# Weight sums of a seven-product block multiplication, made by accumulating transfers

## The chip, the cores and the metric

The kernel runs on one NeuronCore of a Trainium2 chip (trn2). The metric is device time in microseconds of one execution; the median of three runs is compared. The engines are TensorE (PE, with its weight loads shown as PEld), VectorE (DVE), ScalarE (ACT), GpSimd (POOL) and SyncE (SP). Each works through its own queue of instructions in order and waits on semaphores for the others. Transfers are issued by SP, ACT or POOL.

## The reference

One decoder block on x of 512 tokens by 1024 features, in float32: a SwiGLU feed-forward, a token mixer (a gated linear recurrence beside a sliding-window attention), and a second SwiGLU, each with a norm before and behind it.

```python
def swiglu(x, w_gu, w_down):
    g, u = jnp.split(x @ w_gu, 2, axis=-1)
    return (jax.nn.silu(g) * u) @ w_down
...
f = swiglu(rms_norm(h, ffn1_pre_g[l]), ffn1_w_gu[l], ffn1_w_down[l])
h = h + MACARON_SCALE * rms_norm(f, ffn1_post_g[l])
m = hybrid_mixer(rms_norm(h, mix_pre_g[l]), ...)
h = h + rms_norm(m, mix_post_g[l])
f = swiglu(rms_norm(h, ffn2_pre_g[l]), ffn2_w_gu[l], ffn2_w_down[l])
h = h + MACARON_SCALE * rms_norm(f, ffn2_post_g[l])
```

The feed-forward width D_FF is 2816, so `w_gu` is 1024 by 5632. Only the product `x @ w_gu` of the two feed-forwards is touched by the change.

## The kernel before, in words

A float32 product is made of three TensorE products in the type float32r: every operand is split into a high part (a cast to float32r) and a low part (the operand less the high part), and `mm3` (lines 130 to 132) adds high by high, high by low and low by high. ScalarE makes the high parts, VectorE the low parts. A product thus needs the high part of its weights for its first two matmuls and the low part from the third on.

The 22 chunks of 128 gate columns and 128 up columns are made in order. The first 6 chunks of the first feed-forward (names begin with f1) and the first 4 of the second (f2) go through ordinary products of 512 tokens. The rest goes through `paired`, which is where the change lies. `paired` takes a 2 by 2 block form of the multiplication: the features halved on one side, two chunks of 128 columns on the other, and the tokens halved. Seven block products instead of eight give the four result blocks (the form of Strassen and Winograd). The combinations of the moving side (tokens) are made once, in `moving` and `scaled`, and lie in `mv[1]` to `mv[7]`. The combinations of the weights are made for every pair k, from four raw blocks of 128 by 512.

A pair k of chunks is one period. There are n = 16 periods in f1 (an even k makes the gate columns of two chunks, the odd k behind it their up columns) and 18 in f2. A block product is 12 matmuls of 128 by 128 weights on 256 tokens: 4 feature blocks times the three of `mm3`. A period has 7 of them, so 84 matmuls.

In the kernel before, `load(k)` brings the raw blocks as two tiles, L and R (two blocks each, 512 KB each, by SP). `sums(k)` makes four sums on VectorE: M (two blocks), N, and a new first block of L. `parts(k, w)` splits R, M, L and N (w = 1 to 4) into high and low. `product(i, k, start)` issues product i into the PSUM bank X, Y or Q of pair k. Products 1, 6, 3 or 5 and others accumulate on top of each other in one bank, so between them a copy of the bank is taken: `snap` is a ScalarE copy of 256 columns, and `add` is the VectorE addition of such a copy to another bank. `finish` applies the SwiGLU: on an even k (gate) a tanh on ScalarE and a combination on VectorE, on an odd k (up) the multiplication.

`period(k)` is written out by hand and stands under `tc.manual_schedule()`, so the order of the text is what each engine's queue is given. In it products 1, 2, 6 and 7 belong to pair k, and products 5, 3 and 4 to pair k - 1: their weights (parts 3 and 4) are made at the end of a period and used in the next. The low and high parts lie in tiles of the pool `big` (19 buffers), the raw tiles and the part N in `t4p` (8 buffers).

Of the kernel before, what the change touches and what calls it, by code (L numbers as in the profile page):

```python
# [8 lines left out]
F32 = mybir.dt.float32  # L9
# [29 lines left out]
def hybrid_block_kernel(ctx, tc, x, xt, g1, w_first, gains, gu1, gs1, dn1, w_x, w_gate, w_q, w_k, w_v, w_gl, w_ga, w_pl, w_pa,  # L39
# [254 lines left out]
    def paired(fast, name, ps):  # L294
        src, mv = fast
        n = src.shape[0]
        st = [{} for _ in range(n)]
        lo_, hi_ = slice(0, 256), slice(256, 512)

        def load(k):  # L300
            if k < n:
                st[k]["L"], st[k]["R"] = (t4(f"{name}{z}{k}").rearrange("p (a b) -> p a b", a=2) for z in "LR")
                for i, z in ((1, "L"), (0, "R")):
                    SP.dma_start(st[k][z].rearrange("p a b -> p (a b)"), src[k, i])

        def sums(k):
            d = st[k]
            L, R = d["L"], d["R"]
            d["M"] = M = t4(f"{name}M{k}").rearrange("p (a b) -> p a b", a=2)
            d["N"] = N = t2(f"{name}N{k}")  # L310
            for o, a, b in ((M[:, 1], R[:, 1], L[:, 0]), (L[:, 0], L[:, 0], L[:, 1]), (M[:, 0], R[:, 1], L[:, 0]),
                            (N, R[:, 0], M[:, 0])):
                V.tensor_tensor(out=o, in0=a, in1=b, op=ALU.add)

        def parts(k, w):
            d = st[k]
            raw = d["RMLN"[w - 1]]
            if w == 4:
                d["W4"] = t4(f"{name}W4{k}", F32R).rearrange("p (s b) -> p s b", s=2)
            else:  # L320
                d[f"W{w}"] = b8(f"{name}W{w}{k}", [P, 2, 2, 512], F32R)
            t = d[f"W{w}"]
            A.copy(t[:, 0], raw)
            V.tensor_tensor(out=t[:, 1], in0=raw, in1=t[:, 0].bitcast(F32), op=ALU.subtract)  # L324

        def product(i, k, start):
            d = st[k]
            o = d[" XYXQXXQ"[i]][:, lo_]
            w, slot = {1: (1, 1), 2: (1, 0), 3: (4, None), 4: (3, 1), 5: (3, 0), 6: (2, 0), 7: (2, 1)}[i]
            t = d[f"W{w}"]  # L330
            wh, wl = (t[:, 0], t[:, 1]) if slot is None else (t[:, 0, slot], t[:, 1, slot])
            bh, bl = mv[i]
            for k4 in range(4):
                ks = slice(k4 * P, (k4 + 1) * P)
                mm3(o, wh[:, ks], wl[:, ks], bh[:, k4, :], bl[:, k4, :], start and k4 == 0, k4 == 3, True)

        def snap(k, key):
            d = st[k]
            if key == "s1":
                d["sn"] = t2(f"{name}sn{k}")  # L340
                d["s1"], d["s2"] = d["sn"][:, lo_], d["sn"][:, hi_]
            if key == "sW":
                d["sW"] = t2(f"{name}sw{k}")[:, lo_]
            A.copy(d[key], d["X"][:, lo_])  # L344

        def add(k, key):
            d = st[k]
            if key == 11:
                d["a"], d["b"] = t2(f"{name}ca{k}"), t2(f"{name}cb{k}")
                V.tensor_tensor(out=d["a"][:, lo_], in0=d["Y"][:, lo_], in1=d["s1"], op=ALU.add)  # L350
            elif key == 22:
                V.tensor_tensor(out=d["b"][:, hi_], in0=d["Q"][:, lo_], in1=d["sW"], op=ALU.add)
            else:
                V.tensor_tensor(out=d["b"][:, lo_], in0=d["Q"][:, lo_], in1=d["s2"], op=ALU.add)

        def finish(k):
            d = st[k]
            a, b, X = d["a"], d["b"], d["X"][:, lo_]
            j = JSTD[name] + k // 2 * 2
            if k % 2 == 0:  # L360
                d["ta"], d["tb"] = t2(f"{name}ta{k}"), t2(f"{name}tb{k}")
                ta, tb = d["ta"], d["tb"]
                A.activation(ta[:, lo_], a[:, lo_], AF.Tanh, scale=0.5)
                A.activation(ta[:, hi_], X, AF.Tanh, scale=0.5)
                A.activation(tb, b, AF.Tanh, scale=-0.5)
                for o, z in ((ta[:, lo_], a[:, lo_]), (ta[:, hi_], X), (tb, b)):
                    V.scalar_tensor_tensor(out=o, in0=o, scalar=1.0, in1=z, op0=ALU.add, op1=ALU.mult)
            else:
                ta, tb = st[k - 1]["ta"], st[k - 1]["tb"]
                if j % 4 == 0:  # L370
                    ps.append(b8(f"{name}p{j // 4}", [P, 4, T]))
                pa, pb = ps[-1][:, j % 4, :], ps[-1][:, j % 4 + 1, :]
                for o, t, z in ((pa[:, lo_], ta[:, lo_], a[:, lo_]), (pa[:, hi_], ta[:, hi_], X), (pb, tb, b)):
                    V.scalar_tensor_tensor(out=o, in0=t, scalar=0.5, in1=z, op0=ALU.mult, op1=ALU.mult)

        for k in range(3):
            load(k)
        sums(0)
        parts(0, 1)
        parts(0, 2)  # L380

        def period(k):
            c, o, d = k < n, k - 1, k + 1
            if k >= 2:
                add(k - 2, 21)
                finish(k - 2)
            if d < n:
                sums(d)
                parts(d, 1)
# [4 lines left out]
            if o >= 0:  # L394
                product(5, o, False)
            if c:
                snap(k, "s1")
                add(k, 11)
            if o >= 0:
                snap(o, "sW")  # L400
                add(o, 22)
            if c:
                product(6, k, False)
                product(7, k, True)
                if d < n:
                    parts(d, 2)
                snap(k, "s2")
            if o >= 0:
                product(3, o, False)
                product(4, o, False)  # L410
            if c:
                parts(k, 3)
                parts(k, 4)
# [4 lines left out]
            load(k + 3)  # L418
# [575 lines left out]
```

## Time and profile before

| | |
|---|---|
| median of three runs | 1159.44 us (1159.2 to 1159.59) |
| span of the profiled execution | 1158.4 us (its own time beside the span is not on the page) |
| mean granted TensorE clock | 0.995 |
| paired stage of f1 | first matmul 76.9 us, last near 251.5 us |
| paired stage of f2 | first matmul 849.8 us, last near 1036.5 us |
| accumulating transfers, transfers issued by POOL | none |

A row of the timeline reads: start and length in us, engine, line, operation, tile written <- tiles read, sizes, and in brackets the idle time of that engine just before and what ended it. Tile names leave out the numbers: f1X is bank X of any pair, f2W any weight part. A group row has the count behind x, then busy us and the mean in ns of one instruction, then the idle time before them. A row of the transfers ends with the size and the median time from issue to landing. TensorE's instructions overlap: the distance between two starts is the real pace, not the length.

### The profile page before, as it was taken

What the parts mean: (1) busy time and instruction counts of PE and PEld (TensorE: products, weight loads), DVE (VectorE), ACT (ScalarE), POOL (GpSimd) and SP (SyncE); (2) the same over time, 40 slices, a digit from 0 to 9 for tenths busy, and PEclk for the clock granted to TensorE, in tenths of its full rate; (3) what the DMA queues carried; (4) which work ended last, traced back from release to release, by engine and by line L of the source; (5) the groups of instructions that cost most, each with busy time, mean ns of one, the idle gap of its engine ahead of it and who ended that gap; (6) DMA issues with size and microseconds to landing.
All of it is one profiled execution on the core that took longest, in us unless ns stands there. A gap on an engine that the chain in (4) does not pass through costs nothing.

```text
span 1158.4 us, 16623 instructions
## 1 busy us (share of the span) xinstructions
PE 1132.6 (98%) x6680; PEld 1008.4 (87%) x6680; DVE 804.2 (69%) x1182; ACT 537.3 (46%) x924; POOL 57.4 (5%) x58
## 2 busy tenths in 40 slices
PE   7979999999999999999999999999999999999997
PEld 6769999998888988887888888888999999998886
DVE  6598898984415887999877562546769898874303
ACT  7334555553313667566555341425435454553301
POOL 1000000000001010113121000000000000000000
PEclk9999999999999999999999999999999999999999
DMA  9113333284213453622822340624223333274011
GB/s 362 45 66 110 110 110 108 81 297 151 79 54 116 177 139 116 184 72 58 246 84 89 125 163 20 208 83 147 72 74 109 105 101 100 80 272 158 7 37 72
DMA packets 40604, 138.61 MB, mean 120 GB/s; under 512 B 4944, under 2 KB 5072, under 8 KB 39888
## 3 DMA queue, kind: packets, MB, share of 16 engines
q1 hardware_dynamic: 35920, 122.35, 32.4%
q10 hardware_dynamic: 4608, 15.21, 3.7%
q8 instruction: 52, 0.85, 0.3%
q14 instruction: 24, 0.20, 0.1%
HBM read 126.01 MB, written 11.53 MB: 119 GB/s over the span
## 4 chain that ended last, share of the span: by engine, by line
PE 87%; DVE 9%; ACT 2%; issue 2%; DMA 1%; POOL 0%; DVEq 0%; POOLq 0%; ACTq 0%
PE f1o L130 3%; PE f2o L130 3%; PE f1o L132 3%; PE f2o L132 3%; PE f1o L131 3%; PE f2o L131 3%; PE f2X L131 3%; PE f2X L132 3%; PE f2X L130 3%; PE f1X L130 3%; PE f1X L132 3%; PE f1X L131 3%; PE f1f L574 2%; PE f2Q L132 1%; PE f2Q L131 1%
## 5 line engine op out<-in xcount | busy, mean ns | idle before, releaser
L101 DVE TENSOR_TENSOR w<-wraw,w 128x1024 fp32r<-128x1024 f32 x128 | 155.7, 1244 | 67.0 <-ACT w L100 65.6
L100 ACT CAST w<-wraw 128x1024 fp32r<-128x1024 f32 x128 | 129.3, 1049 | 99.7 <-PE f1o L132 17.7
L130 PE MATMUL f1X<-u1m,f1W 128*128 128x256 f32 x256 | 73.1, 286 | 3.7 <-ACT f1sn L344 3.7
L132 PE MATMUL f1X<-u1m,f1W 128*128 128x256 f32 x256 | 73.2, 286 | 2.3 <-DVE f1W L324 2.3
L131 PE MATMUL f1X<-u1m,f1W 128*128 128x256 f32 x256 | 73.0, 285 | 0.0
L130 PE MATMUL f2o<-w,f2ph 128*128 128x512 f32 x176 | 68.6, 390 | 0.0
L130 PE MATMUL f1o<-w,f1ph 128*128 128x512 f32 x176 | 68.5, 390 | 0.0
L131 PE MATMUL f1o<-w,f1ph 128*128 128x512 f32 x176 | 68.5, 389 | 0.0
L131 PE MATMUL f2o<-w,f2ph 128*128 128x512 f32 x176 | 68.5, 389 | 0.0
L132 PE MATMUL f1o<-w,f1pl 128*128 128x512 f32 x176 | 67.0, 389 | 0.0
L132 PE MATMUL f2o<-w,f2pl 128*128 128x512 f32 x176 | 66.9, 389 | 0.0
L130 PEld LDWEIGHTS f1X<-u1m,f1W 128*128 128x128 f32 x256 | 49.6, 194 | 4.0 <-ACT f1sn L344 3.9
L132 PEld LDWEIGHTS f1X<-u1m,f1W 128*128 128x128 f32 x256 | 49.6, 194 | 2.6 <-DVE f1W L324 2.5
L131 PEld LDWEIGHTS f1X<-u1m,f1W 128*128 128x128 f32 x256 | 49.7, 194 | 0.1
L132 PE MATMUL f2X<-u3h,f2W 128*128 128x256 f32 x144 | 40.8, 283 | 0.0
L130 PE MATMUL f2X<-u3m,f2W 128*128 128x256 f32 x144 | 40.8, 283 | 0.0
L131 PE MATMUL f2X<-u3m,f2W 128*128 128x256 f32 x144 | 40.8, 283 | 0.0
L130 PE MATMUL f2Q<-u3m,f2W 128*128 128x256 f32 x144 | 40.8, 283 | 0.0
L131 PE MATMUL f2Q<-u3m,f2W 128*128 128x256 f32 x144 | 40.8, 283 | 0.0
L132 PE MATMUL f2Q<-u3m,f2W 128*128 128x256 f32 x144 | 40.8, 283 | 0.0
L131 PE MATMUL f2X<-u3l,f2W 128*128 128x256 f32 x144 | 40.8, 283 | 0.0
L132 PE MATMUL f2X<-u3m,f2W 128*128 128x256 f32 x144 | 40.7, 283 | 0.0
(722 smaller groups left out, 3519.9 us busy)
## 6 DMA issues: line engine op xcount, KB each, us to landing
wraw<-in_dn_dram SPq DMA_DIRECT2D x44, 512.0 KB, 4.7
f2L<-in_gs_dram SPq DMA_DIRECT2D x18, 512.0 KB, 3.6
f2R<-in_gs_dram SPq DMA_DIRECT2D x18, 512.0 KB, 4.4
wraw<-in_gu_dram SPq DMA_DIRECT2D x16, 512.0 KB, 5.8
f1L<-in_gs_dram SPq DMA_DIRECT2D x16, 512.0 KB, 3.6
f1R<-in_gs_dram SPq DMA_DIRECT2D x16, 512.0 KB, 4.4
wraw<-in_w_x_dram SPq DMA_DIRECT2D x8, 512.0 KB, 4.5
wraw<-in_w_q_dram SPq DMA_DIRECT2D x8, 512.0 KB, 4.4
```

Of the source, the lines that this page charges most:

```text
L100: A.copy(w[:, 0, :], raws[n])
L101: V.tensor_tensor(out=w[:, 1, :], in0=raws[n], in1=w[:, 0, :].bitcast(F32), op=ALU.subtract)
L130: PE.matmul(o, lhsT=ah, rhs=bh, start=start, stop=False, skip_group_check=reopen)
L131: PE.matmul(o, lhsT=ah, rhs=bl, start=False, stop=False, skip_group_check=reopen)
L132: PE.matmul(o, lhsT=al, rhs=bh, start=False, stop=stop, skip_group_check=reopen)
L574: PE.matmul(bs[i], lhsT=lw[:, i * P:(i + 1) * P], rhs=rx, start=k == 0 and n == 0, stop=k == KD - 1 and n == 2)
```

## The change

Only `paired` is changed. The two loaded tiles are now T1 and T2 (the same memory, `src[k, 0]` and `src[k, 1]`), and `sums` is gone. In its place `grow(k, to)` issues from POOL a transfer of one raw block (128 by 512, 256 KB) from HBM that is added, on its way, to a block already in SBUF. Four of them per pair make the four sums S1 to S4:

- to = 1: T2's first block becomes S1, as soon as T2 is loaded;
- to = 2: the same block becomes S2, once S1 has been split;
- to = 3: T1's second block becomes S3, once T1 has been split as it came;
- to = 4: T2's first block becomes S4, once S2 has been split.

So T2's first block holds S1, S2 and S4 one after the other, and each `grow` waits until both engines have read the value before. `parts` now splits A (T1 as it came, 1024 columns) and S1, S2, S3, S4 and A22 (512 columns each) by themselves, where before it was three splits of 1024 columns and one of 512.

The products are reordered. In period k they are now 1, 2, then 4 of pair k - 1, then 5, 6, 3 and 7 of pair k. The banks are X, Y and Z: product 3 accumulates on product 5 in Z, products 1, 6, 7 and 4 in X. Three snaps (s1, s5, s2) and three adds (11, 22, 12) remain. `finish` is cut into two parts, the second for the block that product 4 completes. Loads run two pairs ahead instead of three.

```diff
-        def sums(k):
...
-            for o, a, b in ((M[:, 1], R[:, 1], L[:, 0]), (L[:, 0], L[:, 0], L[:, 1]), (M[:, 0], R[:, 1], L[:, 0]),
-                            (N, R[:, 0], M[:, 0])):
-                V.tensor_tensor(out=o, in0=a, in1=b, op=ALU.add)
+        def grow(k, to):
+            if k < n:
+                z, slot, i, h = {1: ("T2", 0, 1, 1), 2: ("T2", 0, 0, 1), 3: ("T1", 1, 1, 0), 4: ("T2", 0, 0, 0)}[to]
+                G.dma_start(st[k][z][:, slot], src[k, i][:, h * 512:(h + 1) * 512], accum_op=ALU.add)
 
-        def parts(k, w):
+        def parts(k, what):
...
+            raw, hi, lo = {
+                "A": lambda: (d["T1"], d["Wa"][:, 0], d["Wa"][:, 1]),
+                "S1": lambda: (d["T2"][:, 0], d["Wb"][:, 0, 0], d["Wb"][:, 1, 0]),
+                "S2": lambda: (d["T2"][:, 0], d["Wb"][:, 0, 1], d["Wb"][:, 1, 1]),
+                "S3": lambda: (d["T1"][:, 1], d["Wc"][:, 0, 0], d["Wc"][:, 1, 0]),
+                "S4": lambda: (d["T2"][:, 0], d["Wc"][:, 0, 1], d["Wc"][:, 1, 1]),
+                "A22": lambda: (d["T2"][:, 1], d["Wd"][:, 0], d["Wd"][:, 1])}[what]()
+            A.copy(hi, raw)
+            V.tensor_tensor(out=lo, in0=raw, in1=hi.bitcast(F32), op=ALU.subtract)
...
         def product(i, k, start):
             d = st[k]
-            o = d[" XYXQXXQ"[i]][:, lo_]
-            w, slot = {1: (1, 1), 2: (1, 0), 3: (4, None), 4: (3, 1), 5: (3, 0), 6: (2, 0), 7: (2, 1)}[i]
+            o = d[" XYZXZXX"[i]][:, lo_]
+            w, slot = {1: ("Wa", 1), 2: ("Wa", 0), 3: ("Wc", 1), 4: ("Wd", None), 5: ("Wb", 0), 6: ("Wb", 1),
+                       7: ("Wc", 0)}[i]
...
-        for k in range(3):
+        for k in range(2):
             load(k)
-        sums(0)
-        parts(0, 1)
-        parts(0, 2)
+            grow(k, 1)
+        parts(0, "A")
+        grow(0, 3)
+        parts(0, "S1")
+        grow(0, 2)
+        parts(0, "S2")
+        grow(0, 4)
 
         def period(k):
             c, o, d = k < n, k - 1, k + 1
...
+            if o >= 0:
+                add(o, 22)
+                add(o, 12)
             if c:
-                st[k]["X"], st[k]["Y"], st[k]["Q"] = (bank(f"{name}{z}{k}") for z in "XYQ")
+                st[k]["X"], st[k]["Y"], st[k]["Z"] = (bank(f"{name}{z}{k}") for z in "XYZ")
                 product(1, k, True)
+                parts(d, "A")
+                grow(d, 3)
+                snap(k, "s1")
                 product(2, k, True)
+                add(k, 11)
             if o >= 0:
+                product(4, o, False)
+                finish(o, 0)
             if c:
+                parts(d, "S1")
+                grow(d, 2)
+                product(5, k, True)
+                snap(k, "s5")
+                if o >= 0:
+                    finish(o, 1)
+                parts(k, "S3")
                 product(6, k, False)
                 snap(k, "s2")
+                parts(k, "S4")
+                parts(k, "A22")
+                load(k + 2)
+                grow(k + 2, 1)
+                product(3, k, False)
+                parts(d, "S2")
+                grow(d, 4)
+                product(7, k, False)
+            elif o >= 0:
+                finish(o, 1)
...
         period(n)
-        add(n - 1, 21)
-        finish(n - 1)
```

More of the change, by code (lines that the diff above doesn't have):

```diff
@@ L348, in add, with finish @@
             if key == 11:
[L349 to L356, printed above, removed]
+                d["a"], d["b"] = t2(f"{name}ca{k}"), t2(f"{name}cb{k}")[:, lo_]
+            o, z, s = {11: (d["a"][:, lo_], d["Y"], "s1"), 12: (d["a"][:, hi_], d["Z"], "s2"),
+                       22: (d["b"], d["X"], "s5")}[key]
+            V.tensor_tensor(out=o, in0=z[:, lo_], in1=d[s], op=ALU.add)
+        def finish(k, part):
             d = st[k]
@@ L407, in period @@
                 snap(k, "s2")
[L408 to L413, printed above, removed]
+                parts(k, "S4")
[8 more added lines that the diff above has]
+                finish(o, 1)
```

60 lines of the change are left out of this document (19 added, 41 removed).

## The prediction

> **What bounds the kernel now.** I read the page's busy table first, then stretches of the paired stages, then TensorE's waits. Page and stretches:
>
> ```profile
> span 1158.4 us, 16623 instructions
> PE 1132.6 (98%) x6680; PEld 1008.4 (87%) x6680; DVE 804.2 (69%) x1182; ACT 537.3 (46%) x924; POOL 57.4 (5%) x58
> ```
>
> ```profile
> 77.00:100.00 23.00, 16.98 (x127) 16.50 (x126) 21.50 (x29) 10.23 (x16) 0.00 (x0) 0.93 0.22 71
> 100.00:150.00 50.00, 50.00 (x419) 50.00 (x418) 44.91 (x70) 26.32 (x43) 0.00 (x0) 1.00 0.33 105
> 900.00:950.00 50.00, 50.00 (x419) 50.00 (x418) 44.97 (x70) 26.06 (x44) 0.00 (x0) 1.00 0.34 106
> ```
>
> The columns of the second fence, after the stretch, are its length, then PE, PEld, DVE, ACT and POOL busy, the granted clock, the DMA share and GB/s. In the middle of both paired stages 419 matmuls start in 50 us, one per 0.12 us, at full clock. VectorE is busy 45 of 50 us, which is high, but it is not last. TensorE's waits between 77 and 252 us, f1's paired stage, settle that:
>
> ```profile
> PE f1X L130 <- ACT f1sn L344: 3.7, 1, 3.7
> PE f1X L132 <- DVE f1W L324: 2.3, 1, 2.3
> ```
>
> Each happened once, both in the first period. The same list for f2's stage (845 to 1040 us) is empty. So work taken from VectorE there buys almost nothing, and all that a gain could come from is this start:
>
> ```profile
> 77.03 0.28 PE L131 MATMUL f1X<-u1m,f1W 128*128 128x256 f32 x1
> 79.63 0.39 PE L132 MATMUL f1X<-u1m,f1W 128*128 128x256 f32 x1 [2.32 <-DVE f1W L324]
> 79.85 0.28 PE L130 MATMUL f1X<-u1m,f1W 128*128 128x256 f32 x1
> ...
> 86.21 0.58 PE L130 MATMUL f1X<-u1m,f1W 128*128 128x256 f32 x1 [3.70 <-ACT f1sn L344]
> ...
> 89.49 0.28 PE L132 MATMUL f1Q<-u1m,f1W 128*128 128x256 f32 x1
> 89.60 0.28 PE L130 MATMUL f1Q<-u1m,f1W 128*128 128x256 f32 x1
> ```
>
> Behind the 3.70 us wait the matmuls are slow until 89.6: 15 steps take 3.4 us instead of 1.8. So the start loses 2.3 + 3.7 + 1.6 = 7.6 us, which is the largest possible gain.
>
> The rows also show the pattern that decides this change. A product's first two matmuls need only the high part, which ScalarE casts; the third needs the low part, which VectorE subtracts. Here two matmuls passed and the third stood until the subtraction was done.
>
> **The change, part by part.** Rows for prices, from f2's stretch 850 to 1036 us, then one period of it:
>
> ```profile
> L313 DVE TENSOR_TENSOR f2M<-f2R,f2L 128x512 f32<-128x512 f32 x32 | 22.0, 689 | 0.5
> L324 DVE TENSOR_TENSOR f2W<-f2N,f2W 128x512 fp32r<-128x512 f32 x18 | 12.3, 684 | 0.0
> L323 ACT CAST f2W<-f2N 128x512 fp32r<-128x512 f32 x18 | 11.1, 619 | 0.0
> L364 ACT ACTIVATE f2ta<-f2X 128x256 f32<-128x256 f32 x9 | 3.5, 384 | 6.8 <-PE f2X L132 6.8
> ```
>
> ```profile
> 928.72 0.69 DVE L313 TENSOR_TENSOR f2L<-f2L 128x512 f32<-128x512 f32 x1
> 930.58 0.37 ACT L344 COPY f2sw<-f2X 128x256 f32<-128x256 f32 x1 [2.02 <-PE f2X L132]
> 931.70 0.28 PE L132 MATMUL f2X<-u3m,f2W 128*128 128x256 f32 x1
> 931.82 0.28 PE L130 MATMUL f2Q<-u3m,f2W 128*128 128x256 f32 x1
> 932.02 0.37 ACT L344 COPY f2sn<-f2X 128x256 f32<-128x256 f32 x1
> 932.29 1.06 ACT L323 CAST f2W<-f2L 128x1024 fp32r<-128x1024 f32 x1
> ...
> 936.02 0.28 PE L132 MATMUL f2Q<-u3m,f2W 128*128 128x256 f32 x1
> 936.35 0.42 DVE L354 TENSOR_TENSOR f2cb<-f2Q,f2sn 128x256 f32<-128x256 f32 x1 [0.81 <-PE f2Q L132]
> ```
>
> *Sums removed.* Four additions of 0.69 us a period, 2.8 us of VectorE's 9.0 us per 10.08 us. TensorE does not wait for them in steady state: worth 0.
>
> *The order kept.* The queues run as written. The sum that the cast at 932.29 reads was written by 929.4, ScalarE then stood idle for 2.02 us before the copy at 930.58, and the cast still came behind both copies, where the code has it. So I read the new text the same way.
>
> *Product 3 moved (the main term).* Before, the casts of L and N stand behind snap "s2" as well, but products 3, 4 and 5 that use them run a period later. After, the order of period k is product 6, snap "s2", parts "S4", parts "A22", product 3, product 7, all on the same k. Snap "s2" waits for the last matmul of product 6; the S4 cast stands behind it on ScalarE; product 3 needs S4, and product 7 and everything else on TensorE is behind product 3. Nothing covers this. With t the start of product 6's last matmul: the snap starts at t + 0.32 (932.02 less 931.70). The cast starts 0.27 later (932.29 less 932.02), t + 0.59, and takes 0.62: t + 1.21. The hand-overs come from the start of f1:
>
> ```profile
> 78.36 1.21 DVE L324 TENSOR_TENSOR f1W<-f1R,f1W 128x1024 fp32r<-128x1024 f32 x1
> ...
> 85.80 0.36 ACT L344 COPY f1sn<-f1X 128x256 f32<-128x256 f32 x1
> ...
> 89.59 1.05 ACT L323 CAST f1W<-f1L 128x1024 fp32r<-128x1024 f32 x1
> 90.67 1.23 DVE L324 TENSOR_TENSOR f1W<-f1L,f1W 128x1024 fp32r<-128x1024 f32 x1 [1.34 <-ACT f1W L323]
> ```
>
> ScalarE to TensorE 0.05 us (86.16 to 86.21), ScalarE to VectorE 0.03 (90.64 to 90.67), VectorE to TensorE 0.06 (79.57 to 79.63). So product 3 starts at t + 1.26 instead of t + 0.12, the subtraction runs from t + 1.24 to t + 1.92, and its third matmul starts at t + 1.98 instead of t + 0.36. That is 1.62 us of standstill per period. Lower end 1.14 (only ScalarE's part, were the subtraction early), upper end 2.04 (one 256-column instruction of VectorE in the way, 0.42 in the row at 936.35). I take 1.62: by my schedule both engines are free. A product is 12 x 0.12 = 1.44 us, so counted from the start of product 1, product 5's last matmul starts at 5.64 and product 6's at t = 7.08. Snap "s5" starts at 5.96, a tanh (0.38) and the S3 cast (0.62) end by 7.3, before 7.40, where snap "s2" can start. S3's subtraction ends by 7.9, and S4's starts at 8.32.
>
> *Snaps and adds.* Three snaps and three adds as before. Products 1, 2, 4 and 5 read parts made a period earlier or find "s1" taken 4 us before: 0. The tail has one product behind the last period instead of three, the same total: 0.
>
> *Accumulating transfers.* Four a period, 256 KB each, on POOL's queue, which is empty in both stretches. No such transfer is in the trace; the nearest rows are plain ones:
>
> ```profile
> f2L<-in_gs_dram SPq DMA_DIRECT2D x18, 512.0 KB, 3.6
> f2R<-in_gs_dram SPq DMA_DIRECT2D x18, 512.0 KB, 4.4
> ...
> x<-in_x_dram SPq DMA_DIRECT2D x4, 512.0 KB, 8.4
> ...
> out_dram<-b3rh SPq DMA_DIRECT2D x4, 256.0 KB, 2.0
> ```
>
> Call the time from issue to landing, POOL's work on it included, L: between 2.0 and 8.4 us. I take 4.4: an accumulation reads 256 KB twice, as much as one 512 KB load. Is it hidden? The period becomes 10.08 + 1.62 = 11.7. The subtraction of S1(k+1) follows add 11 (product 2's last matmul 2.76 + 0.33, from 936.02 and 936.35), then 0.42 of add and 0.69 + 0.42 of finish, and ends at 5.3; the grow to S2 starts there, its cast and subtraction (1.33) end at 6.6 + L, and the grow to S4 lands at 6.6 + 2L. S4's cast is due at 11.7 + 7.7 = 19.4. So the chain is hidden up to L = 6.4; above that the period is 2L - 1.1. While S2 is late, the next period's A cast and adds are queued behind it on ScalarE and VectorE; product 4 needs add 22 by 14.1 us, which allows L = 7.5. On POOL the grow for k+2 stands ahead of the grow to S4 and waits for its load; SP may issue that when product 4's weights come free (4.4), it lands near 8.8 and the grow to S4 is issued at 11.0. At L = 4.4 all of it costs 0. The DMA share of 0.34 gains once to twice itself, by whether the second read counts; over the longer period that is 0.59 to 0.88, under 1.
>
> *Start of f1.* VectorE has work for 21.5 of the 23 us from 77 on, so the subtraction of A(0) ends about where it does now (79), S1's near 80, and then two transfers of 4.4 us and two pairs of cast and subtraction (1.33 each) follow in a row: S4 is there at 80 + 8.8 + 2.7 = 91.5, six products are through at 91.5 + 22 x 0.12 = 94.1. Before, the same 72 matmuls are through at 93.6 (89.60 starts the 40th, and 33 x 0.12 follow). Plus some slow-clock matmuls (up to 1.6): I take +1.5 for this period, its standstill included; between -3 and +4.
>
> **Sum.** 33 periods (15 of f1, 18 of f2) x 1.62 = 53.5, and 1.5: 55.0. 1158.4 + 55.0 = 1213.4. The page gives the profiled execution only by its span; the median of the three runs is 1159.44, 1.0 above it, so 1214.4.
>
> **Rivals.**
> Transfers late: with L above 6.4 the period is 2L - 1.1. L = 7.5 gives 13.9, 34 x (13.9 - 10.08) = 130 us: 1289. L = 8.4 gives 15.7: 1350. For it: two transfers in series, on the queue of an engine that has issued none so far. Against: loads of twice the written bytes land in 3.6 to 4.4 us. [...]
>
> Clock: idle TensorE may be throttled. After 2.32 us idle the matmuls stayed at 0.12 us, after 3.70 us they ran at about 0.21 and lost 1.6 us. If the new standstill did the same each period, 34 x 1.6 = 54 more: 1269. I give it little since 1.1 and 0.6 us are below the gap that cost nothing. [...]
>
> Not slower: the S4 cast runs ahead of product 6's end, because the queues are not in the written order. Then the standstill is gone, and what is left is the start of f1, at best 7.6 us: 1152. It decides if the S4 cast starts 1.62 us earlier than I have it, by t - 1.03, before product 6 is through. The casts above speak against it.
>
> No difference: both the standstill and the start's gain cancel; I see no rows for it.
>
> **How the numbers follow.** The standstill as worked out 0.68 (its own range 1159.4 + 33 x 1.14 - 3 = 1194 to 1159.4 + 33 x 2.04 + 4 = 1231), late transfers 0.17, clock 0.06, not slower 0.07, no difference 0.02. The range 1194 to 1270 takes in all of the first and the milder part of late transfers (to L = 7.2) and the clock; outside are 0.07 + 0.02 below, and some 0.09 of late transfers above. A measurement of this kernel can tell 0.2% from no change, 2.3 us. Faster 0.07, same 0.02, slower 0.91.
>
> **What would show it.** In f2's middle TensorE waits once or twice a period, in product 3 (tile f2Z), first for ScalarE's cast (f2W) about 1.1 us, then for VectorE about 0.6; the period is near 11.7 us, so about 360 matmuls start in 50 us, at clock 1.00; VectorE falls to about 32 of 50 us. ScalarE's S4 cast stands right behind snap "s2". Late transfers show as casts that wait for a DMA. The prediction is wrong if product 3 starts 0.12 us behind product 6, or if the period is well above 12 us.

## The result, and the profile after

The changed kernel takes 1222.93 us (median of 4 runs, 1220.83 to 1224.45) against 1159.51 for the kernel before (4 runs, 1159.2 to 1160.41): ratio 1.0546, interval 1.0531 to 1.0561, so 5.5% slower. The profiled execution of the changed kernel took 1220.83 us, 1.7 us more than its span and 2.1 us under the median.

Page of the changed kernel, span and busy table:

```profile
span 1219.1 us, 17100 instructions
PE 1148.8 (94%) x6680; PEld 1010.7 (83%) x6680; DVE 729.5 (60%) x1114; ACT 544.5 (45%) x992; POOL 177.2 (15%) x194
```

VectorE has lost 75 us of work and TensorE's share has fallen from 98% to 94%: the time went into gaps between the same 6680 matmuls. The stretches, in the columns used for the kernel before:

```profile
77.00:100.00 23.00, 13.52 (x85) 12.69 (x86) 10.59 (x17) 5.44 (x11) 6.17 (x7) 0.85 0.69 144
100.00:150.00 50.00, 45.19 (x362) 43.55 (x361) 29.37 (x53) 22.81 (x46) 14.95 (x17) 1.00 0.81 170
900.00:950.00 50.00, 45.18 (x362) 43.56 (x361) 29.37 (x51) 21.52 (x44) 14.93 (x17) 1.00 0.83 186
```

A stretch of 50 us lists 362 matmuls where it listed 419, at the same full clock, and the DMA share is 0.83 in place of 0.34. (A stretch also counts the two or three that are under way at its edges. From one product 2 to the next, 925.87 to 937.67 us, a period is 11.80 us; before it was 10.08, from 927.50 to 937.58.) In the first stretch, the start of f1, only 85 are listed in place of 127. TensorE's waits name both places (total us, times, longest us; the list from 60 to 285 us, which holds f1's paired stage):

```profile
PE f1Z L130 <- ACT f1Wc L327: 20.2, 16, 5.5
PE f1Z L132 <- DVE f1Wc L328: 3.4, 15, 0.2
PE f1X L130 <- ACT f1Wb L327: 2.5, 1, 2.5
PE f1X L132 <- DVE f1Wa L328: 1.7, 1, 1.7
```

The first two recur once a period (f1 has 16), in product 3; the two others and the 5.5 us are the start. One period of f2 on TensorE's timeline:

```profile
919.71 0.28 PE L132 MATMUL f2X<-u3m,f2Wb 128*128 128x256 f32 x1
920.97 0.38 PE L130 MATMUL f2Z<-u3h,f2Wc 128*128 128x256 f32 x1 [0.98 <-ACT f2Wc L327]
921.19 0.28 PE L131 MATMUL f2Z<-u3l,f2Wc 128*128 128x256 f32 x1
921.69 0.39 PE L132 MATMUL f2Z<-u3h,f2Wc 128*128 128x256 f32 x1 [0.23 <-DVE f2Wc L328]
921.92 0.28 PE L130 MATMUL f2Z<-u3h,f2Wc 128*128 128x256 f32 x1
```

With t = 919.71, the last matmul of product 6, product 3 starts at t + 1.26 and its third matmul at t + 1.98. ScalarE shows why:

```profile
920.02 0.37 ACT L349 COPY f2sn<-f2X 128x256 f32<-128x256 f32 x1 [0.27 <-PE f2X L132]
920.29 0.62 ACT L327 CAST f2Wc<-f2T 128x512 fp32r<-128x512 f32 x1
920.81 0.62 ACT L327 CAST f2Wd<-f2T 128x512 fp32r<-128x512 f32 x1
922.11 0.62 ACT L327 CAST f2Wb<-f2T 128x512 fp32r<-128x512 f32 x1 [0.68 <-DMA f2T<-in_gs_dram]
```

The S4 cast (920.29) stands behind snap "s2" (920.02), which waits for the last matmul of product 6. The last cast shown waited 0.68 us for a transfer, but product 7 and the next period's first products do not read it, so TensorE saw nothing of it. The transfers and their queue (size in KB, median us from issue to landing; then packets, MB, share of 16 engines' span):

```profile
f2T<-in_gs_dram SPq DMA_DIRECT2D x36, 512.0 KB, 5.5
f2T<-in_gs_dram POOLq DMA_DIRECT2D x72, 256.0 KB, 4.8
```

```profile
q0 software_dynamic: 19584, 35.66, 19.5%
```

### The profile page after: what moved, and what is told of

The parts are those of the page before. It is cut to its first block, busy times and chain, and to the rows that moved or that the text cites. A ratio compares the mean times of both kernels' runs of the same rounds, so it can differ in the third digit from the quotient of the medians.

```text
span 1219.1 us, 17100 instructions
## 1 busy us (share of the span) xinstructions
PE 1148.8 (94%) x6680; PEld 1010.7 (83%) x6680; DVE 729.5 (60%) x1114; ACT 544.5 (45%) x992; POOL 177.2 (15%) x194
## 3 DMA queue, kind: packets, MB, share of 16 engines
q0 software_dynamic: 19584, 35.66, 19.5%
## 4 chain that ended last, share of the span: by engine, by line
PE 82%; DVE 7%; issue 5%; ACT 4%; DMA 1%; POOL 0%; DVEq 0%; POOLq 0%; ACTq 0%
PE f2o L131 3%; PE f1o L131 3%; PE f1o L130 3%; PE f1o L132 3%; PE f2o L130 3%; PE f2o L132 3%; PE f2X L132 3%; PE f2X L131 3%; PE f2X L130 3%; PE f1X L132 2%; PE f1X L130 2%; PE f1X L131 2%; PE f1f L581 2%; PE f2Z L132 2%; PE f1Z L132 2%
## 5 line engine op out<-in xcount | busy, mean ns | idle before, releaser
L309 POOL DMA_DIRECT2D f2T<-in_gs_dram x72 | 63.3, 956 | 178.8 <-DVE f2Wb L328 120.8
L309 POOL DMA_DIRECT2D f1T<-in_gs_dram x64 | 56.5, 958 | 183.2 <-DVE f1Wb L328 98.1
L328 DVE TENSOR_TENSOR f2Wc<-f2T,f2Wc 128x512 fp32r<-128x512 f32 x36 | 24.9, 693 | 24.5 <-ACT f2Wc L327 23.7
L131 PEld LDWEIGHTS f1o<-w,f1ph 128*128 128x128 f32 x176 | 33.0, 188 | 7.2 <-DVE w L101 0.3
L131 PEld LDWEIGHTS f2o<-w,f2ph 128*128 128x128 f32 x176 | 33.0, 188 | 7.0 <-DVE w L101 0.3
L130 PE MATMUL f2Z<-u3h,f2Wc 128*128 128x256 f32 x72 | 22.1, 307 | 17.6 <-ACT f2Wc L327 17.6
L130 PEld LDWEIGHTS f2o<-w,f2ph 128*128 128x128 f32 x176 | 33.0, 188 | 6.9
L132 PEld LDWEIGHTS f1o<-w,f1pl 128*128 128x128 f32 x176 | 33.0, 188 | 6.9
L132 PEld LDWEIGHTS f2o<-w,f2pl 128*128 128x128 f32 x176 | 33.0, 188 | 6.9
L130 PEld LDWEIGHTS f1o<-w,f1ph 128*128 128x128 f32 x176 | 33.0, 188 | 6.7
L328 DVE TENSOR_TENSOR f1Wc<-f1T,f1Wc 128x512 fp32r<-128x512 f32 x32 | 22.2, 692 | 26.0 <-ACT f1Wc L327 25.2
L328 DVE TENSOR_TENSOR f2Wb<-f2T,f2Wb 128x512 fp32r<-128x512 f32 x36 | 24.8, 688 | 17.1 <-ACT f2Wb L327 17.1
```

What stands on the lines that cost most here:

```text
L130: PE.matmul(o, lhsT=ah, rhs=bh, start=start, stop=False, skip_group_check=reopen)
L131: PE.matmul(o, lhsT=ah, rhs=bl, start=False, stop=False, skip_group_check=reopen)
L132: PE.matmul(o, lhsT=al, rhs=bh, start=False, stop=stop, skip_group_check=reopen)
L309: G.dma_start(st[k][z][:, slot], src[k, i][:, h * 512:(h + 1) * 512], accum_op=ALU.add)
L328: V.tensor_tensor(out=lo, in0=raw, in1=hi.bitcast(F32), op=ALU.subtract)
```

## The experiments

The theory under test ("order") is that of the prediction: the loss is the standstill that the new order makes at product 3, plus the start of f1, and the transfers are hidden. The main rival ("transfers") is that the accumulating transfers, or their load on the DMA engines, set the period. Each ratio is against the kernel before on the same chip; its medians lie between 1159.51 and 1159.95 us, so the variants may be compared with each other to some 0.5 us. First the outcome, as a table of order against the way the sums are made (median us):

| | sums by accumulating transfers | sums not formed, no transfers | sums on VectorE |
|---|---|---|---|
| order of the change | 1222.93 | 1210.47 (**no_grow**) | 1215.68 (**dve_sums**) |
| product 4 of the pair before put between 6 and 3 | 1194.2 (**cover**) | 1166.09 (**cover_no_grow**) | 1182.64 (**cover_dve**), 1169.85 (**cover_dve2**) |

**no_grow**: the transfers are left out.

```diff
         def grow(k, to):
-            if k < n:
+            if k < 0:
```

> The accumulating transfers are left out, so the weight sums are not formed (the output is not the reference's); casts, subtractions, products and their order are those of the changed kernel. Order theory: the standstill stays, period 11.7 us, and only the start of f1 gets better (its waits for transfers go, some 6 us): 1210 to 1218. Transfer theory: the period falls to near 10.1 us, 1160 to 1165.

Measured 1210.47 us (1210.31 to 1210.69), ratio 1.0435 (1.0419 to 1.0452). TensorE's waits between 900 and 1000 us, first of this kernel, then of the changed one:

```profile
PE f2Z L130 <- ACT f2Wc L327: 7.8, 8, 1.0
PE f2Z L132 <- DVE f2Wc L328: 2.0, 9, 0.2
```

```profile
PE f2Z L130 <- ACT f2Wc L327: 7.8, 8, 1.0
PE f2Z L132 <- DVE f2Wc L328: 1.8, 8, 0.2
```

They are the same with no accumulating transfer running (DMA share 0.31), and the period is 11.80 us in both. In the steady period the order holds the whole loss. The 12.5 us that the kernel gains lie mostly at f1's start, where 151 matmuls are listed between 77 and 100 us in place of 85: from product 2 of the first pair to that of the second it takes 10.4 us in place of 20.1.

**cover**: one product that needs nothing from the split is put behind product 6, and the part of `finish` that reads its result moves with it.

```diff
             if o >= 0:
-                product(4, o, False)
+                if not c:
+                    product(4, o, False)
                 finish(o, 0)
...
                 snap(k, "s5")
-                if o >= 0:
-                    finish(o, 1)
...
                 snap(k, "s2")
+                if o >= 0:
+                    product(4, o, False)
                 parts(k, "S4")
                 parts(k, "A22")
+                if o >= 0:
+                    finish(o, 1)
```

> Product 4 of the pair before is moved from ahead of product 5 to between products 6 and 3; everything else of the changed kernel stays, its four accumulating transfers per pair too. Order theory: product 4 (1.44 us) covers the cast and the subtraction of S4 (1.62 us of standstill), so 0.1 to 0.4 us of it is left and the period falls from 11.8 to 10.2 to 10.5 us: 1222.9 - 34 x 1.4 = 1175, between 1165 and 1185. Transfer theory (the period is set by how fast the accumulating transfers and loads get through): the transfers took 0.83 of the DMA engines over 11.8 us, 9.8 us a period, or the chain S1, grow, S2, grow, S4 binds; then the period does not fall below 11 us and the time stays above 1195.

Measured 1194.2 us (1189.8 to 1198.6), ratio 1.0282 (1.0257 to 1.0307): between the two forecasts. Stretch 900 to 950, and the one wait of ScalarE for a transfer that stands out between 900 and 1000 us:

```profile
900.00:950.00 50.00, 49.65 (x403) 48.47 (x402) 32.14 (x58) 26.59 (x51) 16.86 (x20) 1.00 0.90 204
```

```profile
ACT f2Wb L327 <- DMA f2T<-in_gs_dram: 19.6, 13, 2.0
```

The standstill is nearly gone (403 matmuls), but with the period near 10.4 us the DMA share is 0.90, and the casts of S1 and S2 wait for transfers, where in the changed kernel they waited 5.2 us from 900 to 1000 us. In this stretch TensorE hardly feels it: the period is 10.36 us, once 10.78, and without the transfers (cover_no_grow, below) it is 10.36 too. It does feel it in f1's first period (20.6 us from product 2 to product 2, against 10.4 without transfers), in eight later ones of f1 (11.5 to 12.5 us; from 150 to 200 us only 359 matmuls are listed) and in four late ones of f2 (11.3 to 12.3). The standstill had hidden the transfers in all periods but f1's first; without it they come through in about a third. Why in these and not in the others stays open.

**cover_no_grow**: cover with the edit of no_grow.

> The order with product 4 between products 6 and 3, and the accumulating transfers left out (the sums are not formed, so the products of the paired stages read other values). Theory 'order and transfers': with the cover run the transfers were what remained of the loss, so without them the time comes near that of before: about 0.25 us a period left of the waits on f2Z (5.1 and 1.6 us in 50 us by that run's rows, less what late transfers caused), 34 x 0.25 = 8 us, less what before itself lost at its start: 1158 to 1166. Rival 'the reordered products or the other PSUM banks cost something beside the two waits': over 1175. Reading that tells them apart: period and matmuls in 50 us (405 or more by the first, under 400 by the second).

Measured 1166.09 us (1166.07 to 1167.13), ratio 1.0058 (1.0044 to 1.0072), 0.1 us above the first theory's range. From 900 to 1000 us the list of TensorE's waits is empty, and a stretch of 50 us lists 408 matmuls. The rest is one late subtraction in product 3 (VectorE has it from 907.78 to 908.47):

```profile
908.22 0.28 PE L131 MATMUL f2Z<-u3l,f2Wc 128*128 128x256 f32 x1
908.53 0.39 PE L132 MATMUL f2Z<-u3h,f2Wc 128*128 128x256 f32 x1
908.75 0.28 PE L130 MATMUL f2Z<-u3h,f2Wc 128*128 128x256 f32 x1
```

The steps are 0.31 and 0.22 instead of 0.12 and 0.12: 0.29 a period, 34 x 0.29 = 9.9 us. Beside it stands what the start no longer loses (160 matmuls from 77 to 100 us, against 127 before; 33 x 0.12 = 4.0). 9.9 - 4.0 = 5.9, and the spans differ by 1164.3 - 1158.4 = 5.9. So nothing else in the new order, the new banks included, has a cost that this balance shows. It can't show one of a microsecond or two: the profiled execution of the kernel before also ran at half the clock from 802.8 to 806.2 us, outside the paired stages, which is up to 1.7 us, and this one did not (mean clock 0.999 against 0.995). From the second column of the table the order costs 1210.47 - 1166.09 = 44.4 us, and the two cells to its left say what the transfers cost: 12.5 us with the standstill, 28.1 without.

**early**: the order of the products stays, but S1's split and its transfer move to the head of the period and S3's and S4's splits stand ahead of product 5.

```diff
                 product(1, k, True)
+                parts(d, "S1")
+                grow(d, 2)
                 parts(d, "A")
...
-                parts(d, "S1")
-                grow(d, 2)
+                parts(k, "S3")
+                parts(k, "S4")
                 product(5, k, True)
...
-                parts(k, "S3")
                 product(6, k, False)
                 snap(k, "s2")
-                parts(k, "S4")
                 parts(k, "A22")
```

> S3 and S4 are split ahead of product 5 instead of behind product 6, and S1 (with its grow) at the start of the period, so that no cast stands behind snap s2 that product 3 needs, and the chain of transfers has its slack back. Order theory: no standstill in a period, 10.1 us as before the change, unless the DMA engines bind (9.8 us of work a period were read from the changed kernel, just under 10.1); with the slower start of f1 1160 to 1172. Transfer theory: the period stays above 11 us, over 1195.

Measured 1208.89 us (1205.68 to 1213.65), ratio 1.0425 (1.0395 to 1.0455). The order theory's number is missed by 37 us. ScalarE between 900 and 1000 us:

```profile
ACT f2Wb L327 <- DMA f2T<-in_gs_dram: 56.0, 16, 6.7
```

ScalarE stands 56 of 100 us in the casts of S1 and S2, up to 6.7 us at a time. The long waits are S1's; its cast is the one that the cast of A (f2Wa, at 940.02) follows:

```profile
939.50 0.62 ACT L327 CAST f2Wb<-f2T 128x512 fp32r<-128x512 f32 x1 [5.59 <-DMA f2T<-in_gs_dram]
```

The edit put this cast at the head of the period, but the transfer that makes S1 is still issued only behind the load, in the period before, and everything on ScalarE is behind the cast. S4's cast, which the edit also asks for earlier, waits 0.72 us (at 942.57). In this order the rival is right: the transfers set the period, 10.9 to 12.7 us between 913 and 997 us. The order of the change leaves them time because it asks for the sums late; for S4, that lateness is the standstill. An order with S4 early and S1 where it was has not been run.

**dve_sums**: the new order, with the four additions back on VectorE (`sums(d)` ahead of `parts(d, "A")`, no `grow`).

> The other half alone: new order and new banks, but the four sums are again made on VectorE (4 x 0.69 us a period) and POOL issues no transfer. Order theory: 1.72 us of standstill in each of 34 periods, 58 us, the start of f1 about as in the kernel before: 1159.5 + 58 = 1217.5, between 1213 and 1224. Transfer theory: the order costs nothing by itself, 1160 to 1165.

Measured 1215.68 us (1215.49 to 1217.68), ratio 1.0486 (1.0472 to 1.05): in the order theory's range. The waits on f2Z are again 7.8 and 1.8 us between 900 and 1000 us. Made on VectorE, the sums cost 7.2 us less than as transfers in this order, and 5.2 more than none; the stretch from 77 to 100 us, with 122 matmuls against 151 in no_grow, holds most of that.

**cover_dve**: dve_sums with the edit of cover.

> Sums on VectorE and product 4 of the pair before between products 6 and 3. If the order alone made the standstill and the transfers alone what was left of it when product 4 covered it (1194 instead of 1175), the period is 10.1 to 10.4 us: 1160 to 1170. If the new order has another cost besides (other banks, more and smaller splits), over 1180.

Measured 1182.64 us (1181.63 to 1183.42), ratio 1.0197 (1.0183 to 1.0211). That is where the second forecast put another cost of the new order. A stretch of 50 us lists 392 matmuls, and the period is 10.73 us. The period still has one wait, and VectorE was never idle ahead of it:

```profile
921.33 0.68 DVE L334 TENSOR_TENSOR f2Wc<-f2N,f2Wc 128x512 fp32r<-128x512 f32 x1
```

```profile
922.07 0.39 PE L132 MATMUL f2Z<-u3h,f2Wc 128*128 128x256 f32 x1 [0.40 <-DVE f2Wc L334]
```

S4's subtraction (921.33) stands in a queue behind S3's, S1's and the finish. So it is VectorE's time and not the banks, which leaves two readings: the order of VectorE's queue, or too much work for it.

**cover_dve2**: the sums and the splits of S1 and S2 are put behind product 3, so behind the splits of S4 and A22, and at the start of a stage the split of A comes ahead of the sums. The diff is against cover_dve.

```diff
-        sums(0)
         parts(0, "A")
+        sums(0)
...
                 product(1, k, True)
-                sums(d)
                 parts(d, "A")
...
-                parts(d, "S1")
                 product(5, k, True)
...
                 product(3, k, False)
+                sums(d)
+                parts(d, "S1")
                 parts(d, "S2")
```

> As cover_dve (sums on VectorE, product 4 between products 6 and 3), with the sums and the splits of S1 and S2 placed behind product 3 and behind the splits of S4 and A22 on VectorE, and the first splits of a stage ahead of its first sums. Theory 'what cover_dve had left, 0.65 us a period, is the order of VectorE's own queue (S4's subtraction stood behind sums)': period 10.1 to 10.4 in place of 10.73, 1160 to 1172. Rival 'VectorE has too little room in the new order, whatever its queue': the wait goes to another tile, 1178 to 1187.

Measured 1169.85 us (1168.74 to 1170.97), ratio 1.0091 (1.0075 to 1.0106): the queue's order it was. The period is 10.36 us, with VectorE as busy as in the kernel before (45 of 50 us):

```profile
900.00:950.00 50.00, 49.83 (x407) 48.82 (x406) 44.98 (x78) 26.15 (x51) 0.00 (x0) 1.00 0.34 106
```

What remains is the same 0.29 us a period as in cover_no_grow, at the same place (steps of 0.31 and 0.23 in product 3).

**a22_first**: the standstill made longer by one cast.

```diff
+                parts(k, "A22")
                 parts(k, "S4")
-                parts(k, "A22")
```

> The two splits behind snap s2 change places: A22 first, then S4. Order theory: ScalarE's cast of A22 (0.52 us from start to start) now also lies between product 6 and product 3, so each of 34 periods grows by 0.5 to 0.6 us: 1222.9 + 18 to 20, 1238 to 1244. Transfer theory: S4 has 0.5 us more for its transfer and nothing is longer: 1220 to 1224.

Measured 1281.37 us (1280.61 to 1281.81), ratio 1.1046 (1.1028 to 1.1063), some 40 us over the order theory's number. TensorE in f2:

```profile
941.26 0.39 PE L130 MATMUL f2Z<-u3h,f2Wc 128*128 128x256 f32 x1 [1.50 <-ACT f2Wc L327]
...
942.08 0.58 PE L132 MATMUL f2Z<-u3h,f2Wc 128*128 128x256 f32 x1 [0.31 <-DVE f2Wc L328]
```

The standstill grew by 0.5 us, as meant, and behind it 15 steps from 942.08 to 945.44 take 3.36 us instead of 1.8. The granted clock is 0.90 from 100 to 200 us, against 1.00 in the changed kernel. That is the prediction's rival "clock", which came here with half a microsecond more; the last section has what the traces show of it.

**plain_pool**: the same transfers from POOL's queue as plain copies (`accum_op` taken away), so the sums are not formed. One run.

> The transfers from POOL copy instead of add (the sums are not formed, the output is not the reference's); all else as in the changed kernel. It prices the addition: if adding doubles the reads and nothing else, the DMA share of the paired stages falls from 0.83 to some 0.55 and the landing from 4.7 to 3 to 4 us; if POOL's descriptor writing and not the addition is what takes the time, share and landing stay. By the order theory the time is that of the kernel without these transfers plus at most the start of f1: 1211 to 1221.

Measured 1215.76 us. Issue to landing, then the queue:

```profile
f2T<-in_gs_dram SPq DMA_DIRECT2D x36, 512.0 KB, 4.4
f2T<-in_gs_dram POOLq DMA_DIRECT2D x72, 256.0 KB, 3.0
```

```profile
q0 software_dynamic: 10880, 35.66, 8.5%
```

The period is that of the changed kernel (11.80 us), and the DMA share is 0.54 to 0.57 in the middle of the paired stages, near the 0.55 expected. No view shows what an addition reads, or what POOL does in an issue. Measured is that for the same 35.66 MB the adding transfer landed in 4.8 us against 3.0, and its packets took 19.5% of 1219.1 us against 8.5% of 1214.0, 2.3 times as much.

**before_k0**: the other way round; the kernel before, with the sums of f1's first pair alone made by transfers, to see if they help where VectorE is late.

```diff
+        def early(k):
...
+            for o in (M[:, 0], M[:, 1]):
+                SP.dma_start(o, blk(0, 1))
+            SP.dma_start(N, blk(0, 0))
+            for o, z in ((M[:, 0], blk(1, 0)), (M[:, 1], blk(1, 0)), (N, blk(0, 1)), (d["L"][:, 0], blk(1, 1)),
+                         (M[:, 0], blk(1, 1)), (N, blk(1, 0)), (N, blk(1, 1))):
+                G.dma_start(o, z, accum_op=ALU.add)
+
         def sums(k):
...
+            if k == 0 and name == "f1":
+                early(k)
+                return
```

> The kernel before, with the sums of f1's first pair alone made by transfers (3 plain copies by SP, 7 accumulating ones by POOL, all in the first 60 us), since that start is the one place where TensorE waits for VectorE. VectorE has 4 additions (2.4 us) less ahead of product 6 of pair 0. If they come out of the 3.70 us wait: 1155.5 to 1157.5, and the wait falls below 1.5 us, so that no slow matmuls follow. If other work of VectorE fills the place: 1158.5 to 1160. If the copies take the room of the weight loads ahead: slower.

Measured 1166.28 us (1164.79 to 1167.43), ratio 1.0057 (1.0044 to 1.0071): slower by 6.7 us. None of the forecasts had the reason. TensorE waits once 9.2 us for ScalarE, and ScalarE's row ahead of that is:

```profile
88.21 1.04 ACT L338 CAST f1W<-f1M 128x1024 fp32r<-128x1024 f32 x1 [12.70 <-DMA f1M<-in_gs_dram]
```

M's first block is a copy and two additions, one behind the other, N's a copy and three; M is there at 88.2 us, while the kernel before cast it at 83.9.

**before_defer**: the kernel before, with the sums and first split of f1's second pair moved behind the first pair's work, in the first period only.

```diff
-            if d < n:
+            late = k == 0 and name == "f1"
+            if d < n and not late:
                 sums(d)
                 parts(d, 1)
...
                 snap(k, "s1")
                 add(k, 11)
+            if late:
+                parts(d, 1)
+                sums(d)
```

> The kernel before, with one edit in the first period of f1: the sums of its second pair and the splits of its next period's S1 come after product 2, the subtraction of M(0) and the A11 updates, not ahead of product 1. Theory 'the first period of f1 waits on VectorE, whose queue holds the second pair's sums, themselves waiting for a transfer, ahead of M(0)': product 6 of the first period starts about 3 us earlier, and with the stop shorter fewer matmuls run at the lower clock after it: gain of 3 to 4.5 us, 1155 to 1157. Rival 'the VectorE work only moves, or the transfer that it waits for sets the time all the same': 1158.5 to 1160.5.

Measured 1157.02 us (10 runs, 1156.38 to 1157.61) against 1159.81 (14 runs), ratio 0.9975 (0.9966 to 0.9985): 2.8 us faster than the kernel before, just short of the forecast 3 to 4.5.

```profile
78.74 0.38 PE L132 MATMUL f1X<-u1m,f1W 128*128 128x256 f32 x1 [2.32 <-DVE f1W L324]
83.17 0.38 PE L130 MATMUL f1X<-u1m,f1W 128*128 128x256 f32 x1 [1.54 <-ACT f1sn L344]
84.16 0.58 PE L132 MATMUL f1X<-u1m,f1W 128*128 128x256 f32 x1 [0.49 <-DVE f1W L324]
```

Product 6 starts at 83.17 in place of 86.21. The slow matmuls did not go: they now follow 84.16.

**before_defer2**: before_defer, and the first split of M in two halves behind the copy of product 1's bank.

```diff
                 snap(k, "s1")
+                if late:
+                    t = st[k]["W2"] = b8(f"{name}W2{k}", [P, 2, 2, 512], F32R)
+                    for s in range(2):
+                        raw = st[k]["M"][:, s]
+                        A.copy(t[:, 0, s], raw)
+                        V.tensor_tensor(out=t[:, 1, s], in0=raw, in1=t[:, 0, s].bitcast(F32), op=ALU.subtract)
                 add(k, 11)
```

> As before_defer, and the first split of M in f1 comes in two halves (product 6 reads the first alone), behind the copy of product 1's bank on ScalarE instead of ahead of it. Theory 'what is left of the stop in f1's first period is the order on ScalarE and the size of one split': in before_defer M's first half is summed by 81.7, product 6 starts at 83.17 and its third matmul at 84.16; here the half cast ends by 82.4 and the half subtraction by 83.2, so the third matmul starts near 83.2 less what else moved: 1 us earlier. If the lower clock is set off by the sum of idle time within a few us (1.54 + 0.49 us in before_defer, 1.50 + 0.31 in a22_first, not 0.98 + 0.23 in the changed kernel), the stop here, about 0.8 + 0.5 us, stays below it and the 17 slow matmuls go too, 1.5 us more: 1154 to 1155. If the clock drops all the same (the 2.32 us wait just before counts with it): 1155.5 to 1156.3. Rival 'VectorE's other work sets the time': 1156.5 to 1157.5, as before_defer.

Measured 1156.89 us (1156.3 to 1157.61), ratio 0.9977 (0.9968 to 0.9987): no different from before_defer. The number is the rival's, but none of the mechanisms came as I had them. The waits of product 6 are gone, but the clock dropped earlier, and two small waits came in the next period:

```profile
80.08 0.49 PE L132 MATMUL f1X<-u1m,f1W 128*128 128x256 f32 x1 [2.32 <-DVE f1W L324]
...
90.95 0.39 PE L130 MATMUL f1X<-u1m,f1W 128*128 128x256 f32 x1 [0.64 <-ACT f1W L323]
...
92.20 0.39 PE L132 MATMUL f1X<-u1m,f1W 128*128 128x256 f32 x1 [0.76 <-DVE f1W L324]
```

The same 2.32 us wait that cost no clock in the kernel before and in before_defer was followed here by 16 slow steps at once (80.08 to 83.56).

## Why the prediction came out as it did

The direction and the mechanism were right, and 1222.93 lies in the range and 8.5 us above the number. Step by step:

- **Product 3 moved.** Right: t + 1.26 and t + 1.98 were forecast and measured, in the two waits named, and no_grow, dve_sums and cover_no_grow show that it is the order and not the transfers. The size was short by 0.10 us a period: the step behind the last wait takes 0.23 (921.69 to 921.92) where I counted 0.12, so the standstill is 1.72. It was in the quoted rows already, 79.63 to 79.85. The two periods bear it out, 11.80 - 10.08 = 1.72. 33 x 0.10 = 3.3 us.
- **Start of f1.** This is the step that failed most: +1.5 forecast, 4.7 measured. TensorE's rows for the end of its longest wait and for the 73rd matmul:

```profile
92.77 0.58 PE L130 MATMUL f1Z<-u1m,f1Wc 128*128 128x256 f32 x1 [5.53 <-ACT f1Wc L327]
...
98.21 0.28 PE L130 MATMUL f1X<-u1m,f1Wa 128*128 128x256 f32 x1
```

The first six products are through at 98.21 in place of 93.56. The 24 steps between the rows take 5.44 us instead of 2.88: the lower clock cost 2.6 here, where I had put up to 1.6. VectorE finished S1's subtraction at 78.75, sooner than the 80 that I took. But the two transfers in a row, from the end of the subtraction that frees the block to the cast that reads the sum, took 5.6 and 6.4 us (78.75 to 84.39, 85.73 to 92.10) instead of 4.4 each, of which POOL's own issue is 0.88, with two issues in a row both times:

```profile
78.45 1.77 POOL L309 DMA_DIRECT2D f1T<-in_gs_dram  x2 [15.51 <-DVE f1Wa L328]
...
86.03 1.77 POOL L309 DMA_DIRECT2D f1T<-in_gs_dram  x2 [2.62 <-DVE f1Wb L328]
```

no_grow bears it out: without accumulating transfers neither of the two waits for ScalarE ahead of products 6 and 3, 2.5 and 5.5 us, is there, and its first period has no more than its standstill. Its span is 50.2 above that of before. The count gives 34 x 1.72 = 58.5, plus 1.7 for the wait in its first product, less the 7.6 that the kernel before lost at its start: 52.6. Up to 1.7 of the 2.4 between them is the slow stretch of the kernel before at 802.8 us.

- **The sum.** 56.8 + 4.7 = 61.5 against 60.7 between the two spans. Of the 8.5 us by which the median misses, 3.3 are the restart, 3.2 the start and 2.8 the distance of the median from the profiled span (3.8, where I had 1.0); the terms together are 0.8 too large. The slow stretch of the kernel before at 802.8 us, up to 1.7, is in none of them, so the sum is good to a microsecond or two and no better.
- **Accumulating transfers.** 4.8 and 4.6 us to landing in the two stages, where 4.4 was taken out of 2.0 to 8.4 (the time of a 512 KB load; an estimate, as no run shows what an addition reads); hidden in the steady period, as forecast. DMA share 0.81 to 0.83, in the forecast 0.59 to 0.88 and near its top, so here an added byte did count for more than a plain one (2.3 times, 19.5% against 8.5% of the span, by plain_pool). What I did not say is that the cover was the standstill itself: cover, in about a third of its periods, and early, in most, show that the same transfers set the time in another order. The limit L = 6.4 was worked out for this order alone.
- **Sums removed.** 0, as forecast: dve_sums puts the additions back and shows the same waits in f2.
- **Clock.** Given 0.06 and argued away by gaps that had cost nothing. It did not come in the periods (clock 1.00), but the argument was weak: a22_first shows it with 1.50 and 0.31 us idle, well below the 2.32 us on which I leaned.
- **Not slower** and **no difference**: the S4 cast did run behind snap "s2", in the written order.

## What to carry to other kernels

When work is reordered, follow one product's inputs through each engine's queue from the last matmul that releases them: the standstill here could be read to 0.1 us from rows of the kernel before, and one independent product in the gap took most of it away (1.72 to 0.29 us a period in cover_no_grow). Work on an engine that nobody waits for was worth nothing here in steady state (the waits on f2Z are 7.8 and 1.8 us in 100 us with the sums on VectorE and with the transfers), and the same engine can be the last one in the first period of a stage, where moving later pairs' work back gained what there was (0.25%). An operation that is hidden has to be priced again for each new order, because its cover may be the very stall that the next edit removes.

## What the hardware showed unexpectedly

- The accumulating transfers took 2.3 times the DMA engines' time of plain copies of the same bytes (19.5% against 8.5% of the span for 35.66 MB; the changed kernel against one run of plain_pool), in 19584 packets against 10880, and landed in 4.8 us against 3.0 for 256 KB; the loads beside them took longer too (512 KB in 5.5 us against 4.4). POOL was busy for 0.96 us with an issue (mean of f2's 72), against 0.55.

- In these runs the length of a wait alone does not tell when TensorE's clock drops. In a22_first the same 1.50 and 0.31 us did nothing in one period and were followed by the lower clock in the next:

```profile
914.96 0.39 PE L130 MATMUL f2Z<-u3h,f2Wc 128*128 128x256 f32 x1 [1.50 <-ACT f2Wc L327]
915.77 0.39 PE L132 MATMUL f2Z<-u3h,f2Wc 128*128 128x256 f32 x1 [0.31 <-DVE f2Wc L328]
...
927.37 0.39 PE L130 MATMUL f2Z<-u3h,f2Wc 128*128 128x256 f32 x1 [1.50 <-ACT f2Wc L327]
928.18 0.43 PE L132 MATMUL f2Z<-u3h,f2Wc 128*128 128x256 f32 x1 [0.31 <-DVE f2Wc L328]
```

Behind 915.77 no slow step follows; behind 928.41 16 steps to 931.82 take 3.41 us. One wait of 2.32 us likewise did nothing in two kernels and stood ahead of the drop in a third, while 0.98 and 0.23 us (changed kernel, clock 1.00 in both stretches) had none behind them. Four drops had one length: 3.36 us in a22_first at 942.08 and 3.41 at 928.41, 3.37 in before_defer (84.16 to 87.53), 3.48 in before_defer2 (80.08 to 83.56).

The granted clock in the traces says more. In the kernel before and in the changed one it is either 1.00 or 0.50. Ahead of the kernel's end it drops at 86.03 and 802.83 us of the kernel before, for 3.41 us each, and at 91.15 us of the changed kernel, for 6.83 us, twice as long. The two drops of the kernel before are 716.80 us apart, 210 times 3.413, and the slow steps of a22_first begin again 13.67 us after 928.41, some four times 3.41. So I read the traces in stretches of 3.41 us, laid off from a drop, and ask how long TensorE stood idle in each. That is a reading of these drops and not a mechanism that a view shows. In a22_first the first two rows hold the waits of 914.96 and 915.77, the third those of 927.37 and 928.18, and the fourth is the drop:

```profile
911.34:914.75 3.41, 2.13 (x18) 1.92 (x17) 1.40 (x3) 2.14 (x5) 1.75 (x2) 1.00 0.37 49
914.75:918.16 3.41, 2.89 (x22) 2.68 (x23) 1.66 (x3) 1.73 (x3) 0.66 (x1) 1.00 0.81 180
924.99:928.40 3.41, 1.60 (x11) 1.20 (x10) 2.41 (x4) 2.71 (x7) 0.70 (x1) 1.00 0.84 124
928.40:931.81 3.41, 3.41 (x17) 3.41 (x17) 0.69 (x1) 0.92 (x1) 0.87 (x1) 0.50 0.95 298
```

TensorE is idle for 1.28 and 0.52 us of the first two, and for 1.81 of the third. In the kernel before and in the changed one, read so from 62 us on, the stretches at full clock that have a drop behind them have 3.41, 1.91 and 3.08 us idle (kernel before, from 82.62, 799.42 and 1150.99) and 3.41 and 2.89 (changed kernel, from 87.74 and 1210.73); the longest idle times without one are 1.89 (kernel before, from 75.79), 1.77 and 1.50 (changed kernel, from 80.91 and 828.43). So 1.81 and 1.91 us had a drop behind them, 1.77 and 1.89 had none, and what decides there these traces do not show. The 2.32 us wait lies across the edge at 79.20 in the kernel before. As an estimate from where the slow steps end, it lies across an edge in before_defer too (87.53, so edges near 77.3 and 80.7, the wait from 76.42 to 78.74) and whole in one stretch in before_defer2 (83.56, so edges near 76.7 and 80.2, the wait from 77.76 to 80.08). In the paired stages of the changed kernel, behind the first period of f1, no stretch has more than 1.20 us idle, and none has a drop behind it.
